# One more pair as seven products, one bank through four of them, the sums' first loads on another queue, and a reordered opening

## The chip, the cores and the metric

The kernel runs on one core of a Trainium2 chip. The time is the device time in microseconds (us) of one execution. It was measured in three runs. One further execution was recorded by the profiler, and everything that is said below of single instructions comes from that record.

The engines are named as the profile names them: PE is the matrix engine (TensorE), PEld its weight loads, DVE the vector engine, ACT the scalar engine, POOL the GpSimd engine, and SP the engine that here only issues DMAs. Each has its own queue of instructions and works it off in order. A DMA is issued by an instruction of some engine (SPq, POOLq, ACTq in the profile) and lands later; who needs its data waits for its semaphore.

## The reference

The reference is two layers of an encoder with width 1024 over 512 positions, all float32. In each layer four token mixers (latent attention, a Fourier transform, differential attention, a gated linear recurrence) run beside each other on one normalized input, their results are gated, summed and projected into the residual. Then comes the part that this case is mostly about, the feed-forward network (FFN) of width 2816:

```python
for l in range(DEPTH):                       # 2 layers
    ...
    h2 = rmsnorm(x, ln_ffn[l])
    ...
    x = x + (jax.nn.silu(g_part) * u_part) @ w_down[l]
```

`g_part` and `u_part` are the two halves of `h2 @ w_gate_up[l]`.

## The kernel before

The activations are kept transposed, as 8 tiles of 128 channels x 512 positions. Every float32 factor is split into two parts, `hi` and `lo`, in a format that PE multiplies fast: ACT writes `hi`, DVE writes `lo` as the difference (`split`, lines 121 and 122). A product is then three matmuls, hi x hi, hi x lo and lo x hi (lines 141 to 143 for a plain gemm, line 1066 for the seven products).

**Opening.** SP loads the first weight `hf00` in two cuts with `x` tile 0 between them, then the seven other x tiles, then the second weight `hf01` and more. The first gemm (`hf00`) consumes the x tiles as they come and are split into `hhm` and `hlm`. Then come `hf01`, `hq0`, `hg0`. `ssx` (line 188) is the sum of squares for the norm, two matmuls of true float32.

**FFN.** The 22 column tiles of the gate and the 22 of the up projection go as 22 pairs `j`. The string `SEVEN` says how pair j is computed:

- "8", an ordinary pair (`eight`): two gemms of 8 k-tiles x 3 matmuls of 128x512, so 48 matmuls.
- "7" (`seven`): the pair is seen as a 2 x 2 block product (gate and up columns by the two halves of the channels, times two halves of the channels by two halves of 256 positions) and is computed with seven products instead of eight, in the manner of Strassen and Winograd. Each product is 4 k-tiles x 3 matmuls of 128x256, so 84 matmuls in all. The products are named by what moves through PE: `T1` to `T4` are sums of the activations, made once for each layer (`right_sums`), and `B11`, `B21`, `B22` are plain blocks. The stationary factors are the weights `a11`, `a12`, `a22` and the sums of weights `s1` to `s4`.

`sums(j)` makes the weights of a seven. Three loads on SP bring `wr_f` (512 KB, two blocks), `s31` (512 KB, the first half of a sum) and `a22` (256 KB). One load on POOL then adds 512 KB more onto `s31` in memory (`accum_op`), so that `s31` holds two sums. It has to wait until the first load of `s31` has landed. From there DVE makes `s24` with two adds, and five splits follow: `one` (of `wr_f`, 1024 wide), `v24` (of `s24`, 1024 wide), `v1` and `v3` (the two halves of `s31`), and `v22` (of `a22`). `s31` has two buffers, so the load for pair j + 2 waits until the last reader of pair j's `s31` is done. In the trace `s31`, `s24` and so on are named without their numbers: `s_f` is `s31_f` and `s24_f`, `a_f` is `a22_f`, `vh_f` and `vl_f` are the hi and lo of the 512-wide splits, `wh_f` and `wl_f` of the 1024-wide ones.

The results of a seven go through three PSUM banks, `fa` (`r1`), `fb` (`r2`) and `fc` (`r3`). P1 below is the product of `a11` and P2 that of `a12`. The last two products of a seven, T4 and B22, with what follows (`finish`), are put off into the next seven, where `rest()` calls them. `hidden` multiplies gate and up and splits the result into `ah` and `al`. After 8, 8 and 6 pairs comes a piece of the down projection: eight gemms (`d`) over the pairs of the block.

The order in which instructions stand in each engine's queue is made by a scheduler from the order of the program and from priorities: `tc.high_priority(AHEAD)` in `sums` and `weight` moves loads and splits forward by 156 places. What stands where is fixed when the program is built, not at run time.

Of the kernel before, what the change touches and what calls it, by code (L numbers as in the profile page):

```python
# [11 lines left out]
F32 = mybir.dt.float32  # L12
# [16 lines left out]
LOG_EXP = "natural_log_exp_and_others"  # L29
WL, WR = 3, 2  # L30
LAYERS = range(L)
SEVEN = "8888887777777777777777"
AHEAD = 156
ORDER = "ccbccchhhchhcbchcghcchcchzccczccbccccccchgcgccchbbbcbhcgbzcbbcbccbgghcbgcgcbcccghchghchzhbccccbccccgcccccczhgcgbgchcgcccccccggggggbgcggggbcbbggcbbcbhcccbccbccccccccccccccccccbchccgbgggbchcbbbbbbhbbb"
PE = 8
PM = 4
# [26 lines left out]
def body(tc, io):  # L63
# [7 lines left out]
    with pool("const") as cl, pool("hp") as hp, pool("wp", WL) as wp, pool("vals", side="right") as cp, \  # L71
# [2 lines left out]
            pool("pq", 2, space=bass.MemoryType.PSUM) as pq:  # L74


        ident = cl.tile([P, P], F32, name="ident")
        make_identity(nc, ident)
        ones = cl.tile([P, P], F32, name="ones")
        V.memset(ones, 1.0)  # L80
        blk64 = cp.tile([P, P], F32, name="blk64")
        V.memset(blk64, 0.0)
        V.memset(blk64[0:64, 0:64], 1.0)
# [5 lines left out]
        xpool = [None]  # L89
        x = []  # L90

        def load_x(src, who):
            xpool[0] = pool(f"x{who}", side="right")
            px = xpool[0].__enter__()
            x[:] = [px.tile([P, S], F32, name=f"x{who}_{k}") for k in range(KD)]
            return [lambda k=k: nc.sync.dma_start(x[k], src[k]) for k in range(KD)]

        def drop_x():
            xpool[0].__exit__(None, None, None)
# [2 lines left out]
        def tmp(shape, tag="t", dt=F32, bufs=None, name="t"):  # L102
            return tp.tile(shape, dt, tag=tag, name=name, bufs=bufs)
# [21 lines left out]
            A.activation(hi, src, AF.Copy, scale=g)  # L125
            V.scalar_tensor_tensor(lo, src, g, hi.bitcast(F32), op0=ALU.mult, op1=ALU.subtract)

        def weight(src, n, name, cuts=(), between=None):
            raw = rp.tile([P, 1024], F32, tag="wr", name=f"wr_{name}")
            hi = wp.tile([P, 1024], F32R, tag="wh", name=f"wh_{name}")  # L130
            lo = wp.tile([P, 1024], F32R, tag="wl", name=f"wl_{name}")
            with tc.high_priority(AHEAD):
                for a, b in zip((0,) + cuts, cuts + (n,)):
                    nc.sync.dma_start(raw[:, a:b], src[:, a:b])
                    split(hi[:, a:b], lo[:, a:b], raw[:, a:b])
                    if between:
                        between.pop()()
            return hi, lo
# [87 lines left out]
        xs = nc.dram_tensor("x_mid", (KD, P, S), F32).ap()  # L226
        for l in LAYERS:
            lam_init = 0.8 - 0.6 * math.exp(-0.3 * l)
            pk = cp.tile([P, PK_N], F32, tag="pk", name=f"pk{l}")
            tc.keep_in_program_order(nc.scalar.preload_act_table_set(LOG_EXP))  # L230
            nc.scalar.dma_start(pk, io["pk"][l])


            if l == LAYERS[0]:
                with tc.high_priority(1000):
                    loads = load_x(io["x"], "in")
                    w0 = weight(io["w_z"][l, 0], 1024, "hf00", (256,), [loads[1], loads[0]])
                    for load in loads[2:]:
                        load()
            else:  # L240
                w0 = weight(io["w_z"][l, 0], 1024, "hf00")
            with pool(f"mo{l}") as mo, pool(f"mx{l}") as mp:
                hh, hl, scale, normed = prenorm(pk[:, PK_MIX:PK_MIX + 8], f"m{l}")
                first = [gemm(None, hh, hl, "hf00", w0)]
                r = scale()
                for c, name in ((1, "hf01"), (4, "hq0"), (6, "hg0")):
                    first.append(gemm(io["w_z"][l, c], hh, hl, name))
                sig0 = mp.tile([P, 3, S], F32, name="sig0")
                for j in range(2):
                    mul(sig0[:, j], first[j], r)  # L250
# [769 lines left out]
            with pool(f"fa{l}") as fa, pool(f"ff{l}") as fp, ps_pool(f"fr{l}", 2) as fr:  # L1020
# [48 lines left out]
                def sums(j):  # L1069

                    src = io["w_gu"][l, j]
                    with tc.high_priority(AHEAD):
                        raw = rp.tile([P, 1024], F32, tag="wr", name=f"wr_f{j}")
                        nc.sync.dma_start(raw, src[:, :1024])
                        s31 = fp.tile([P, 1024], F32, tag="s31", name=f"s31_f{j}", bufs=2)
                        nc.sync.dma_start(s31, src[:, 512:1536])
                        a22 = fp.tile([P, 512], F32, tag="a22", name=f"a22_f{j}", bufs=2)
                        nc.sync.dma_start(a22, src[:, 1536:])  # L1080
                        nc.gpsimd.dma_start(s31, src[:, 1024:], accum_op=ALU.add)

                        def pair(src, n):
                            if n == 1024:
                                hi = wp.tile([P, n], F32R, tag="wh", name=f"wh_f{j}")
                                lo = wp.tile([P, n], F32R, tag="wl", name=f"wl_f{j}")
                            else:
                                hi = fp.tile([P, n], F32R, tag="vh", name=f"vh_f{j}", bufs=4)
                                lo = fp.tile([P, n], F32R, tag="vl", name=f"vl_f{j}", bufs=4)
                            split(hi, lo, src)  # L1090
                            return hi, lo

                        one = pair(raw, 1024)
# [24 lines left out]

                def seven(j):
                    a11, a12, a22, s1, s2, s3, s4 = sums(j)  # L1120
                    gs = fp.tile([P, S], F32, tag="gs", name="gs")
                    us = fp.tile([P, S], F32, tag="us", name="us", bufs=2)
                    r1 = acc_psum(f"fa{j}")
                    product(r1, a11, B11, True)
                    c1 = tmp([P, H], "ps", name="c1")
                    A.activation(c1, r1[:, :H], AF.Copy)
                    rest()
                    r2 = fr.tile([P, S], F32, tag="r2", name=f"fb{j}")
                    r3 = acc_psum(f"fc{j}")
                    uu = tmp([P, 2, H], "n0", name="uu", bufs=1)  # L1130
                    product(r2, s2, T2, True)
                    add(uu[:, 0], c1, r2[:, :H])
                    product(r3, s1, T1, True)
                    product(r1, a12, B21, False)
                    A.activation(gs[:, :H], r1[:, :H], AF.Silu)
                    product(r2, s3, T3, False)
                    add(uu[:, 1], c1, r2[:, :H])
                    add(us[:, H:], uu[:, 1], r3[:, :H])

                    def finish():  # L1140
                        product(r2, a22, T4, False)
                        add(us[:, :H], c1, r2[:, :H])
                        product(r3, s4, B22, False)
                        add(gs[:, H:], uu[:, 0], r3[:, :H])
                        A.activation(gs[:, H:], gs[:, H:], AF.Silu)
                        hidden(j, gs, us, -1.0)

                    left.append(finish)

                def eight(j):  # L1150

                    t = [fp.tile([P, S], F32, tag=n, name=n, bufs=b) for n, b in (("gs", 1), ("us", 2))]
                    pr = []
                    for i in range(2):
                        if 2 * j + i < len(raw):
                            mul(t[i], raw[2 * j + i], r)
                            pr.append(t[i])
                        else:
                            pr.append(gemm(half_gu(2 * j + i), hh, hl, f"f{2 * j + i}"))
                        rest()  # L1160
                    A.activation(t[0], pr[0], AF.Silu)
                    if pr[1] is not t[1]:
                        mul(t[1], pr[1], t[0])
                        ah[j] = fa.tile([P, S], F32R, tag=f"ah{j % 8}", name=f"ah{j}")
# [148 lines left out]
```

## Time and profile before

| | us |
|---|---|
| median of 3 runs | 1725.94 (1723.2 to 1726.93) |
| profiled execution, its time | 1724.95 |
| profiled execution, its span | 1723.2 |
| PE busy | 1697.8 |
| PEld busy | 1422.5 |
| DVE busy | 1179.0 |
| ACT busy | 808.8 |
| POOL busy | 43.0 |

The span runs from the first to the last instruction; the time of an execution also holds what lies around it. A row of a time order has the start, the duration, the engine, the line, the operation with its output, an arrow and its inputs, the shape, the count, and in brackets the idle time ahead of it with the instruction that ended it. A group of instructions has its total busy time and the mean in ns. The chain of work that ended last is followed back from the last instruction. A row of DMA issues ends in the time from issue to landing.

### The profile page before, as it was taken

The numbers are of one execution on the slowest core, as the hardware profiler recorded it, in microseconds if no ns is written. First come the engines' busy times: TensorE is split into PE (matmuls) and PEld (weight loads), VectorE is DVE, ScalarE is ACT, GpSimd is POOL, SyncE is SP. The second block draws the span as 40 slices with busy tenths as digits, with TensorE's granted clock in tenths as the row PEclk, the third lists the DMA queues.
The fourth block names the chain that finished last, engine by engine and source line by source line (L and its number), as shares of the span: only waits on it lengthen the run. The fifth ranks groups of instructions, "written<-read, shape, count | busy, mean of one in ns | idle before, by whom it ended". The sixth has DMA issues, their size and how long they took to land.

```text
span 1723.2 us, 25722 instructions
## 1 busy us (share of the span) xinstructions
PE 1697.8 (99%) x10220; PEld 1422.5 (83%) x10220; DVE 1179.0 (68%) x1979; ACT 808.8 (47%) x1352; POOL 43.0 (2%) x68
## 2 busy tenths in 40 slices
PE   8999999999999999999999999999999999999999
PEld 6787778877787989989887777788777788899897
DVE  8858775457769647748677687754667695487473
ACT  7374353456555424525453743534564453254251
POOL 1000000000000000000000000000000000000000
PEclk9999999999999999999999999999999999999999
DMA  5222203332262435644442221142323624365443
GB/s 193 64 80 86 74 26 115 105 99 86 87 201 100 138 110 161 170 122 126 133 136 58 87 74 62 43 119 97 110 75 111 189 87 140 118 177 145 127 115 104
DMA packets 62473, 191.58 MB, mean 111 GB/s; under 512 B 7953, under 2 KB 9361, under 8 KB 62353
## 3 DMA queue, kind: packets, MB, share of 16 engines
q1 hardware_dynamic: 56304, 170.10, 30.4%
q0 software_dynamic: 5760, 19.42, 6.2%
q8 instruction: 80, 1.31, 0.3%
q10 hardware_dynamic: 288, 0.43, 0.1%
q14 instruction: 41, 0.33, 0.1%
HBM read 179.42 MB, written 4.19 MB: 107 GB/s over the span
## 4 chain that ended last, share of the span: by engine, by line
PE 87%; DVE 7%; ACT 3%; DMA 2%; issue 1%; SPq 0%; POOLq 0%; ACTq 0%; DVEq 0%
PE fb L1066 8%; PE g L142 6%; PE g L141 6%; PE g L143 6%; PE fc L1066 5%; PE fa L1066 5%; PE d L141 5%; PE d L143 5%; PE d L142 5%; PE f L142 3%; PE f L141 3%; PE f L143 3%; DMA s_f<-in_w_gu 2%; PE av L942 1%; PE sm L909 1%; PE hf L142 1%
## 5 line engine op out<-in xcount | busy, mean ns | idle before, releaser
L141 PE MATMUL g<-hhm,wh_g 128*128 128x512 f32 x512 | 202.0, 394 | 0.0
L143 PE MATMUL g<-hhm,wl_g 128*128 128x512 f32 x512 | 201.5, 394 | 0.0
L142 PE MATMUL g<-hlm,wh_g 128*128 128x512 f32 x512 | 201.5, 394 | 0.0
L143 PE MATMUL d<-ah,wl_d 128*128 128x512 f32 x352 | 136.9, 390 | 0.5 <-DVE wl_d L122 0.5
L141 PE MATMUL d<-ah,wh_d 128*128 128x512 f32 x352 | 137.2, 392 | 0.0
L142 PE MATMUL d<-al,wh_d 128*128 128x512 f32 x352 | 137.1, 390 | 0.0
L122 DVE TENSOR_TENSOR wl_g<-wr_g,wh_g 128x1024 fp32r<-128x1024 f32 x64 | 78.3, 1223 | 73.8 <-ACT wh_g L121 73.8
L121 ACT ACTIVATE wh_g<-wr_g 128x1024 fp32r<-128x1024 f32 x64 | 67.7, 1058 | 115.4 <-PE g L142 80.1
L142 PEld LDWEIGHTS g<-hlm,wh_g 128*128 128x128 f32 x512 | 96.3, 188 | 20.4 <-issue 1.5
L141 PEld LDWEIGHTS g<-hhm,wh_g 128*128 128x128 f32 x512 | 96.3, 188 | 20.2 <-issue 0.8
L143 PEld LDWEIGHTS g<-hhm,wl_g 128*128 128x128 f32 x512 | 96.3, 188 | 20.0 <-issue 0.8
L121 ACT ACTIVATE wh_d<-wr_d 128x1024 fp32r<-128x1024 f32 (+1 forms) x48 | 47.5, 989 | 111.7 <-PE d L142 85.5
L118 DVE TENSOR_TENSOR xm<-xm,d 128x512 f32<-128x512 f32 x48 | 33.0, 688 | 88.9 <-PE d L143 88.8
L121 ACT ACTIVATE wh_f<-wr_f 128x1024 fp32r<-128x1024 f32 x50 | 53.0, 1059 | 79.1 <-PE d L142 35.0
L121 ACT ACTIVATE vh_f<-s_f 128x512 fp32r<-128x512 f32 x64 | 40.1, 630 | 103.4 <-PE fb L1066 63.8
L910 DVE TENSOR_REDUCE nm<-sm 128x1 f32<-128x512 f32 x64 | 43.8, 689 | 51.3 <-PE sm L909 50.9
L143 PEld LDWEIGHTS d<-ah,wl_d 128*128 128x128 f32 x352 | 66.1, 188 | 14.9 <-DVE wl_d L122 1.4
L141 PEld LDWEIGHTS d<-ah,wh_d 128*128 128x128 f32 x352 | 66.0, 188 | 14.9 <-ACT ah L121 1.9
L142 PEld LDWEIGHTS d<-al,wh_d 128*128 128x128 f32 x352 | 66.1, 188 | 14.0 <-DVE al L122 1.2
L1066 PE MATMUL fb<-th,vh_f 128*128 128x256 f32 x256 | 75.7, 296 | 0.4 <-DVE uu L118 0.3
L1066 PE MATMUL fa<-hhf,wl_f 128*128 128x256 f32 x256 | 72.7, 284 | 0.0
L1066 PE MATMUL fa<-hlf,wh_f 128*128 128x256 f32 x256 | 72.5, 283 | 0.0
(444 smaller groups left out, 4845.6 us busy)
## 6 DMA issues: line engine op xcount, KB each, us to landing
wr_g<-in_w_g SPq DMA_DIRECT2D x64, 512.0 KB, 3.6
wr_f<-in_w_gu SPq DMA_DIRECT2D x50, 512.0 KB, 3.5
s_f<-in_w_gu SPq DMA_DIRECT2D x32, 512.0 KB, 4.5
s_f<-in_w_gu POOLq DMA_DIRECT2D x32, 512.0 KB, 5.4
wr_d<-in_w_d SPq DMA_DIRECT2D x32, 512.0 KB, 3.5
wr_b<-in_w_b SPq DMA_DIRECT2D x16, 512.0 KB, 3.4
wr_o<-in_w_o SPq DMA_DIRECT2D x16, 512.0 KB, 3.5
a_f<-in_w_gu SPq DMA_DIRECT2D x32, 256.0 KB, 3.0
```

Of the source, the lines that this page charges most:

```text
L118: V.tensor_tensor(out, a, b, op=ALU.add)
L121: A.activation(hi, src, AF.Copy)
L122: V.tensor_tensor(lo, src, hi.bitcast(F32), op=ALU.subtract)
L141: T.matmul(ps, lh, rh, start=first, stop=False)
L142: T.matmul(ps, lh, rl, start=False, stop=False)
L143: T.matmul(ps, ll, rh, start=False, stop=last)
L909: T.matmul(ps, qs[0:96, t * P:(t + 1) * P], ks[0:96], start=True, stop=True)
L910: V.tensor_reduce(nm[:, j:j + 1], ps, axis=AX.X, op=ALU.max, negate=True)
L942: T.matmul(av[e * 64:e * 64 + 64], vv[:, b, 2 * i + e], pts[i][e][:, b].rearrange("p t q -> p (t q)"), start=t == 1 and b == 0, stop=b == ...
L1066: T.matmul(ps[:, :H], lh[:, c], rh, start=first and k == 0 and n == 0, stop=k == Q - 1 and n == 2, skip_group_check=True)
```

## The change

1. `SEVEN` has five ordinary pairs at its start instead of six, so each layer has 17 sevens.
2. In `seven` P1 goes into `fb` (before: `fa`), and its result is copied by ACT (`c1`). P2 goes alone into `fa`, and DVE adds `c1` for the first half of the gate. Then come T4 and B22 of the pair before. T2, T3 and T4 go on accumulating on `fb`, and after each of them ACT copies what it holds (`cc[:, 0]`, `cc[:, 1]` and the first half of `us`). DVE adds that to what is in `fc`. In before, the four sums were made by DVE adds with `c1` (`uu`). Additions on DVE that read PSUM go from 5 to 3 in each seven, and what ACT reads of PSUM or of their result (copies and `silu`) from 3 to 6.
3. `gs` has two buffers instead of one, `us` one instead of two.
4. The first load of `s31` is issued by POOL, ahead of its accumulating load.
5. The opening: constants and the parameters `pk` come first, ten matmuls of a tile of ones with itself (`early`, 128x128, true float32) run first on PE, and SP loads the weight `hf01` in two cuts among the x tiles, in a fixed order.

The core of the diff:

```diff
-SEVEN = "8888887777777777777777"
+SEVEN = "8888877777777777777777"
+EARLY = 10
...
+        ones = cl.tile([P, P], F32, name="ones")
+        V.memset(ones, 1.0)
+        early = pq.tile([P, S], F32, tag="sc", name="early")
+        for _ in range(EARLY):
+            T.matmul(early[:, :P], ones, ones, start=True, stop=True)
...
-                    loads = load_x(io["x"], "in")
-                    w0 = weight(io["w_z"][l, 0], 1024, "hf00", (256,), [loads[1], loads[0]])
-                    for load in loads[2:]:
-                        load()
+                    loads = load_x(io["x"], "in", tc.keep_in_program_order)
+                    some = lambda *ks: lambda: [loads[k]() for k in ks]
+                    w0 = weight(io["w_z"][l, 0], 1024, "hf00", (256,), [some(1, 2, 3), some(0)],
+                                tc.keep_in_program_order)
+                    w1 = weight(io["w_z"][l, 1], 1024, "hf01", (512,), [some(6, 7), some(4, 5)],
+                                tc.keep_in_program_order)
...
-                        nc.sync.dma_start(s31, src[:, 512:1536])
+                        nc.gpsimd.dma_start(s31, src[:, 512:1536])
...
-                    gs = fp.tile([P, S], F32, tag="gs", name="gs")
-                    us = fp.tile([P, S], F32, tag="us", name="us", bufs=2)
+                    gs = fp.tile([P, S], F32, tag="gs", name="gs", bufs=2)
+                    c1 = tmp([P, H], "ps", name="c1")
                     r1 = acc_psum(f"fa{j}")
-                    product(r1, a11, B11, True)
-                    c1 = tmp([P, H], "ps", name="c1")
-                    A.activation(c1, r1[:, :H], AF.Copy)
+                    r2 = fr.tile([P, S], F32, tag="r2", name=f"fb{j}")
+                    product(r2, a11, B11, True)
+                    A.activation(c1, r2[:, :H], AF.Copy)
+                    product(r1, a12, B21, True)
+                    add(gs[:, :H], c1, r1[:, :H])
+                    A.activation(gs[:, :H], gs[:, :H], AF.Silu)
                     rest()
-                    r2 = fr.tile([P, S], F32, tag="r2", name=f"fb{j}")
+                    cc = tmp([P, 2, H], "n0", name="cc", bufs=1)
                     r3 = acc_psum(f"fc{j}")
-                    uu = tmp([P, 2, H], "n0", name="uu", bufs=1)
-                    product(r2, s2, T2, True)
-                    add(uu[:, 0], c1, r2[:, :H])
+                    product(r2, s2, T2, False)
+                    A.activation(cc[:, 0], r2[:, :H], AF.Copy)
                     product(r3, s1, T1, True)
-                    product(r1, a12, B21, False)
-                    A.activation(gs[:, :H], r1[:, :H], AF.Silu)
                     product(r2, s3, T3, False)
-                    add(uu[:, 1], c1, r2[:, :H])
-                    add(us[:, H:], uu[:, 1], r3[:, :H])
+                    A.activation(cc[:, 1], r2[:, :H], AF.Copy)
+                    us = fp.tile([P, S], F32, tag="us", name="us")
+                    add(us[:, H:], cc[:, 1], r3[:, :H])

                     def finish():
                         product(r2, a22, T4, False)
-                        add(us[:, :H], c1, r2[:, :H])
+                        A.activation(us[:, :H], r2[:, :H], AF.Copy)
                         product(r3, s4, B22, False)
-                        add(gs[:, H:], uu[:, 0], r3[:, :H])
+                        add(gs[:, H:], cc[:, 0], r3[:, :H])
```

The scheduler then puts the instructions in another order. DVE's queue between two sevens in the second block of a layer stood so in before; a row has the line, the operation, the output, an arrow, the inputs and the shape, `f12` is pair 12, and the last number of a name tells buffers apart:

```order
L122 TENSOR_TENSOR vl_f11_6277<-s31_f11_6256,vh_f11_6276 128x512
L122 TENSOR_TENSOR al9_6196<-us_6017,ah9_6195 128x512
L122 TENSOR_TENSOR wl_f11_6269<-s24_f11_6265,wh_f11_6268 128x1024
L122 TENSOR_TENSOR vl_f11_6281<-a22_f11_6258,vh_f11_6280 128x512
L118 TENSOR_TENSOR s24_f12_6399<-s31_f12_6390,wr_f12_6388 128x512
L118 TENSOR_TENSOR uu_6201<-c1_6165,fb10_6199 128x256
L118 TENSOR_TENSOR s24_f12_6399<-s24_f12_6399,wr_f12_6388 128x512
L118 TENSOR_TENSOR us_6151<-uu_6201,fc10_6200 128x256
```

and stands so now:

```order
L1128 SCALAR_TENSOR_TENSOR us_6201<-us_6201,gs_6098 128x512
L126 TENSOR_TENSOR s24_f12_6484<-s31_f12_6475,wr_f12_6473 128x512
L126 TENSOR_TENSOR s24_f12_6484<-s24_f12_6484,wr_f12_6473 128x512
L130 TENSOR_TENSOR vl_f11_6361<-s31_f11_6340,vh_f11_6360 128x512
L130 TENSOR_TENSOR al9_6293<-us_6201,ah9_6292 128x512
L130 TENSOR_TENSOR vl_f11_6365<-a22_f11_6342,vh_f11_6364 128x512
L126 TENSOR_TENSOR us_6336<-cc_6296,fc10_6297 128x256
L126 TENSOR_TENSOR gs_6368<-c1_6369,fa11_6370 128x256
```

The first row of the first piece is `v3` of pair 11, the last reader of `s31_f11`; it stood ahead of the two sums `s24` of pair 12 and stands behind them now. The add into `us` that reads bank `fc10` comes behind both in both.

The queues that issue the loads of a seven: before, on SP

```order
L1076 DMA wr_f12_6388<-in_w_gu 128x1024
L1078 DMA s31_f12_6390<-in_w_gu 128x1024
L1080 DMA a22_f12_6392<-in_w_gu 128x512
L1076 DMA wr_f13_6522<-in_w_gu 128x1024
L1078 DMA s31_f13_6524<-in_w_gu 128x1024
L1080 DMA a22_f13_6526<-in_w_gu 128x512
```

with the accumulating loads alone on POOL (line 1081), and now, on POOL:

```order
L1092 DMA s31_f11_6340<-in_w_gu 128x1024
L1095 DMA s31_f11_6340<-in_w_gu 128x1024
L1092 DMA s31_f12_6475<-in_w_gu 128x1024
L1095 DMA s31_f12_6475<-in_w_gu 128x1024
L1092 DMA s31_f13_6610<-in_w_gu 128x1024
L1095 DMA s31_f13_6610<-in_w_gu 128x1024
```

Line 1092 is the plain load and 1095 the accumulating one. Both are now in one queue, pair by pair, and SP keeps `wr_f` and `a22`.

At the start of the program SP's queue is now this, where before `hf01` stood behind all eight x tiles (`xin`) as one load:

```order
L142 DMA wr_hf00_119<-in_w_z 128x256
L104 DMA xin_0_111<-in_x 128x512
L142 DMA wr_hf00_119<-in_w_z 128x768
L104 DMA xin_1_112<-in_x 128x512
L104 DMA xin_2_113<-in_x 128x512
L104 DMA xin_3_114<-in_x 128x512
L142 DMA wr_hf01_132<-in_w_z 128x512
L104 DMA xin_4_115<-in_x 128x512
L104 DMA xin_5_116<-in_x 128x512
L142 DMA wr_hf01_132<-in_w_z 128x512
L104 DMA xin_6_117<-in_x 128x512
L104 DMA xin_7_118<-in_x 128x512
```

The two cuts of `hf01` come behind x tiles 3 and 5, and the last x tile is the last of them.

More of the change, by code (lines that the diff above doesn't have):

```diff
@@ L74, in body @@
             pool("pq", 2, space=bass.MemoryType.PSUM) as pq:
+        pk0 = cp.tile([P, PK_N], F32, tag="pk", name=f"pk{LAYERS[0]}")
+        tc.keep_in_program_order(nc.scalar.dma_start(pk0, io["pk"][LAYERS[0]]))
+        tc.keep_in_program_order(nc.scalar.preload_act_table_set(LOG_EXP))
+        ones = cl.tile([P, P], F32, name="ones")
[3 more added lines that the diff above has]
+            T.matmul(early[:, :P], ones, ones, start=True, stop=True)
         ident = cl.tile([P, P], F32, name="ident")
         make_identity(nc, ident)
-        ones = cl.tile([P, P], F32, name="ones")
-        V.memset(ones, 1.0)
         blk64 = cp.tile([P, P], F32, name="blk64")
@@ L90, in body, with load_x @@
         x = []
-        def load_x(src, who):
+        def load_x(src, who, keep=lambda i: i):
             xpool[0] = pool(f"x{who}", side="right")
@@ L95, in load_x @@
             x[:] = [px.tile([P, S], F32, name=f"x{who}_{k}") for k in range(KD)]
-            return [lambda k=k: nc.sync.dma_start(x[k], src[k]) for k in range(KD)]
+            return [lambda k=k: keep(nc.sync.dma_start(x[k], src[k])) for k in range(KD)]
         def drop_x():
@@ L126, in split_g, with weight @@
             V.scalar_tensor_tensor(lo, src, g, hi.bitcast(F32), op0=ALU.mult, op1=ALU.subtract)
-        def weight(src, n, name, cuts=(), between=None):
+        def weight(src, n, name, cuts=(), between=None, keep=lambda i: i):
             raw = rp.tile([P, 1024], F32, tag="wr", name=f"wr_{name}")
@@ L133, in weight @@
                 for a, b in zip((0,) + cuts, cuts + (n,)):
-                    nc.sync.dma_start(raw[:, a:b], src[:, a:b])
+                    keep(nc.sync.dma_start(raw[:, a:b], src[:, a:b]))
                     split(hi[:, a:b], lo[:, a:b], raw[:, a:b])
@@ L228, in body @@
             lam_init = 0.8 - 0.6 * math.exp(-0.3 * l)
-            pk = cp.tile([P, PK_N], F32, tag="pk", name=f"pk{l}")
-            tc.keep_in_program_order(nc.scalar.preload_act_table_set(LOG_EXP))
-            nc.scalar.dma_start(pk, io["pk"][l])
+            if l == LAYERS[0]:
+                pk = pk0
+            else:
+                pk = cp.tile([P, PK_N], F32, tag="pk", name=f"pk{l}")
+                tc.keep_in_program_order(nc.scalar.preload_act_table_set(LOG_EXP))
+                nc.scalar.dma_start(pk, io["pk"][l])
             if l == LAYERS[0]:
                 with tc.high_priority(1000):
-                    loads = load_x(io["x"], "in")
-                    w0 = weight(io["w_z"][l, 0], 1024, "hf00", (256,), [loads[1], loads[0]])
-                    for load in loads[2:]:
-                        load()
+                    loads = load_x(io["x"], "in", tc.keep_in_program_order)
[4 more added lines that the diff above has]
+                                tc.keep_in_program_order)
             else:
+                w1 = None
                 w0 = weight(io["w_z"][l, 0], 1024, "hf00")
@@ L246, in body @@
                 for c, name in ((1, "hf01"), (4, "hq0"), (6, "hg0")):
-                    first.append(gemm(io["w_z"][l, c], hh, hl, name))
+                    first.append(gemm(io["w_z"][l, c], hh, hl, name, w1 if c == 1 else None))
                 sig0 = mp.tile([P, 3, S], F32, name="sig0")
@@ L1150, in eight @@
                 def eight(j):
-                    t = [fp.tile([P, S], F32, tag=n, name=n, bufs=b) for n, b in (("gs", 1), ("us", 2))]
+                    t = [fp.tile([P, S], F32, tag=n, name=n, bufs=b) for n, b in (("gs", 2), ("us", 1))]
                     pr = []
```

## The prediction

> **What bounds the kernel now.** I read the page first, then the chain of work that ended last, then the time order of PE, DVE and the queues in the FFN.
>
> ```profile
> span 1723.2 us, 25722 instructions
> PE 1697.8 (99%) x10220; PEld 1422.5 (83%) x10220; DVE 1179.0 (68%) x1979; ACT 808.8 (47%) x1352; POOL 43.0 (2%) x68
> PE 87%; DVE 7%; ACT 3%; DMA 2%; issue 1%; SPq 0%; POOLq 0%; ACTq 0%; DVEq 0%
> ```
>
> TensorE (PE) is the bound, with 87% of the chain. So an edit gains only what it takes out of PE's own row of matmuls, and it loses whatever makes PE wait. POOL issues few instructions, among them the accumulating loads of the sevens. The FFN of the chain shows the unit of work:
>
> ```profile
> 669.00 1.44 PE fa L1066 x12
> 670.43 1.44 PE fb L1066 x12
> 671.88 1.44 PE fa L1066 x12
> 673.32 3.00 PE fb L1066 x23
> ```
>
> One product of twelve 128x256 matmuls takes 1.44 us, so a "seven" is 7 x 1.44 = 10.08 us of PE.
>
> **The change, part by part.**
>
> *One more seven per layer.* An "eight" is two gemms of 24 matmuls 128x512. The next rows give their spacing, and they serve the opening too:
>
> ```profile
> 6.59 0.79 PE L141 MATMUL hf<-hhm,wh_hf 128*128 128x512 f32 x1 [6.59 <-ACT hhm L125]
> 12.99 0.59 PE L142 MATMUL hf<-hlm,wh_hf 128*128 128x512 f32 x1
> 13.41 0.40 PE L143 MATMUL hf<-hhm,wl_hf 128*128 128x512 f32 x1
> 20.24 1.02 PE L188 MATMUL ssx<-ss,ones 128*128 128x512 f32 x2
> 22.25 0.39 PE L141 MATMUL hq<-hhm,wh_hq 128*128 128x512 f32 x1
> 23.84 0.39 PE L142 MATMUL hq<-hlm,wh_hq 128*128 128x512 f32 x1
> ```
>
> From 22.25 to 23.84 are seven steps, 0.227 each; an eight is 48 x 0.227 = 10.89 us. A pair gains 0.81 and there is one per layer: **-1.6 us**.
>
> *The fourth product's wait.* In before, T4 writes the bank `fb` that the DVE add into `uu` still reads. The add stands in DVE's queue behind weight sums, so T4 starts late in every seven. The first and the last place with a gap ahead of T4, in time order, and the groups of the page:
>
> ```profile
> 588.38 0.28 PE L1066 MATMUL fb<-th,wh_f 128*128 128x256 f32 x1
> 588.58 0.38 PE L1066 MATMUL fb<-th,vh_f 128*128 128x256 f32 x1
> 1675.38 0.28 PE L1066 MATMUL fb<-tl,wh_f 128*128 128x256 f32 x1
> 1675.59 0.39 PE L1066 MATMUL fb<-th,vh_f 128*128 128x256 f32 x1
> L1066 PE MATMUL fb<-th,vh_f 128*128 128x256 f32 x256 | 75.7, 296 | 0.4 <-DVE uu L118 0.3
> L1066 PE MATMUL fa<-hlf,wh_f 128*128 128x256 f32 x256 | 72.5, 283 | 0.0
> ```
>
> A late first matmul is longer, and over 32 sevens the group of T3 and T4 is 75.7 - 72.5 = 3.2 us above its equal. The gap ahead of it is 0.2 instead of 0.12, in sixteen such places from 588 to 1675, some 2.3 us with the larger ones (0.48 at most). Together 5.5 us. In the change T4 waits for an ACT copy made right after T3, and P1 and P2 of the next pair (2.88 us) lie between. The copy costs about this:
>
> ```profile
> 671.67 0.36 ACT L1135 ACTIVATE gs<-fa 128x256 f32<-128x256 f32 x1
> 671.93 0.62 ACT L121 ACTIVATE vh_f<-a_f 128x512 fp32r<-128x512 f32 x1
> 673.35 0.38 ACT L1126 ACTIVATE c<-fa 128x256 f32<-128x256 f32 x1 [0.80 <-PE fa L1066]
> ```
>
> Three more copies are 1.1 us per seven on an engine that is 47% busy. They are hidden, but T3 waits for the copy of T2 with only T1's 1.44 us between, and a copy that lands behind a 1.06 us split would use that up. I take **-5 us**, with bounds 0 and -5.5.
>
> *The opening.* PE runs at 0.427 per matmul (6.41 over 15 from 6.59 to 12.99) and at 0.227 from 13.41. The second gemm's weight came last, so 24 of its matmuls and the ssx pair (1.0 us) stand behind the first gemm, and hq starts at 22.25. The bytes up to there are the same in the change (3.1 MB):
>
> ```profile
> 6.00:13.00 7.00, 6.41 (x14) 4.30 (x15) 6.40 (x10) 7.00 (x12) 0.00 (x0) 1.00 1.03 393
> ```
>
> At 393 GB/s they still end at about 12.3; x7 then comes last, and its split ends near 13.9. By then the two gemms have run interleaved, and some 18 matmuls (4.1 us) and ssx (1.0 us) are left, so hq starts at about 19.0, a gain of 3.3 if the clock is open by then. The ten early matmuls take about 0.43 each (estimate from the slow spacing), 4.3 us in all, and can run before the first data comes, that is before 6.59. If they bring the clock forward only partly the gain is about 2.2, and 0 if nothing moves. I take **-2.8**.
>
> [...]
>
> *The first load of `s31` on POOL's queue.* This decides the forecast. Each seven needs a sum loaded in two steps, a plain 512 KB load and an accumulating one that waits for the first to land:
>
> ```profile
> 660.34 0.33 SPq L1078 DMA_DIRECT2D s_f<-in_w_gu  x1
> 665.15 0.86 POOL L1081 DMA_DIRECT2D s_f<-in_w_gu  x1 [10.37 <-DVE us L118]
> s_f<-in_w_gu SPq DMA_DIRECT2D x1, 512.0 KB, 4.3
> s_f<-in_w_gu POOLq DMA_DIRECT2D x1, 512.0 KB, 5.4
> s_f<-in_w_gu SPq DMA_DIRECT2D x32, 512.0 KB, 4.5
> s_f<-in_w_gu POOLq DMA_DIRECT2D x32, 512.0 KB, 5.4
> ```
>
> The single-issue rows belong to the two issues above them: 660.34 + 4.3 = 664.6 landed, 0.55 later POOL issues, and 5.4 later the sum is there: 10.2 us per pair of loads. In before this hides, because DVE reads in this order:
>
> ```profile
> 670.07 0.69 DVE L122 TENSOR_TENSOR vl_f<-s_f,vh_f 128x512 fp32r<-128x512 f32 x1
> 670.78 0.33 SPq L1078 DMA_DIRECT2D s_f<-in_w_gu  x1
> 673.55 0.68 DVE L118 TENSOR_TENSOR s_f<-s_f,wr_f 128x512 f32<-128x512 f32 x1
> 674.48 0.68 DVE L118 TENSOR_TENSOR s_f<-s_f,wr_f 128x512 f32<-128x512 f32 x1
> ```
>
> The last reader of pair n's buffer (the v3 split, 670.07) ends, SP reloads it at once (670.78) for pair n+2, and only then come the sums of pair n+1 (673.55). In the changed order DVE does the sums of n+1 **first**, then v3 of n. With two buffers that closes a loop: sums of n+1 wait for their loads, v3 of n waits behind them, the loads for n+2 wait for v3 of n, and the sums of n+2 wait for those. One turn costs:
> - sums and v3 on DVE: 0.2 to notice the landing, 0.6 + 0.6 + 0.69 by the rows' spacing: 2.1 us
> - release to issue: 0.05 (670.76 to 670.78 on SP; up to 0.55 on POOL)
> - landing to the next issue 0.55, the accumulating load 5.2 (5.4 and 5.0 in the two single-issue rows)
> - the plain load on POOL. Before doesn't show it for this tile. Of these two rows, the first is of all `s_f` loads on both queues, the second of the only plain loads of this size that POOL issues, `dft`, four of 516 KB, two at a time; the third is a single accumulating one:
>
> ```profile
> DMA to landing us min/median/max: 3.0/5.1/10.2
> DMA to landing us min/median/max: 3.9/4.5/4.9
> s_f<-in_w_gu POOLq DMA_DIRECT2D x1, 512.0 KB, 5.0
> ```
>
> The lower end for it is 3.0 (SP's best), the upper 4.9. I take 4.0, near the shortest of POOL's own, since here it is alone but for a 256 KB load.
>
> The sum is 2.1 + 0.05 + 4.0 + 0.55 + 5.2 = **11.9 us a turn**, against 10.08 of PE work. Behind v3 on DVE stand the al and v22 splits and the add that empties bank `fc`, for which PE's B22 waits: 3.7 us after the sums can start. Walk a block of eight sevens, with its first product at 0. The first seven has no predecessor to finish (7.2 us), then each takes 10.08, so B22 of the second, third and fourth seven is due at 21.6, 31.7 and 41.8. Ahead of the adds that release them stand the sums of the fourth, fifth and sixth seven, which so must start by 17.9, 28.0 and 38.1. v3 of the second seven goes into the buffer that T1 of the first reads until 4 x 1.44 = 5.8; with 0.2 to notice, 0.62 on ACT and 0.69 on DVE it ends at 7.3. So the fourth sums start at 7.3 + 9.8 = 17.1 (in time), the fifth at 29.0 (1.0 late), and every later one 1.8 further behind. The late places are the sums of the last four sevens: 1.0 + 3 x 1.8 = 6.5. A block of six has 1.0 + 1.8 = 2.8; the first block's three sevens have none. That is 9.3 per layer, **+18.6 us**. Bounds: turns of 10.6 or less give 0; 11.3 gives about 9; 12.5 (the plain load at 4.5) about 28; 12.9 (at 4.9) about 34.
>
> [...]
>
> SP's queue only loses a load per seven, and on POOL nothing stands behind these waits but the loads of the next seven.
>
> Sum, against the profiled execution's own 1724.95 (1.75 above its span, 1.0 below the median of 1725.94): 1724.95 - 1.6 - 5 - 2.8 + 18.6 = **1734.2 us**.
>
> **The rivals.**
> - *The loads keep up* (not slower). Point of decision: a turn of 10.6 us. If the plain load on POOL takes SP's shortest 3.0 and the accumulating one its shortest 5.0, a turn is 2.1 + 0.05 + 3.0 + 0.55 + 5.0 = 10.7, and the loop costs under 1 us: 1724.95 - 9.4 + 0 to 1 = 1715.5 to 1716.5. For it: in before SP's load is asked for 1.2 us behind a `wr_f` load of 512 KB and is slowed by it, and in the change it isn't. Against it: the four POOL loads never took under 3.9.
> - *Just over*: a turn near 11.2 to 11.4, with 7 to 11 us of stall: 1722.5 to 1727, no change that could be told.
> - *The loads crowd each other*: a turn of 12.3 to 12.9, since SP's `wr_f` and `a_f` loads run beside both, and the DVE order leaves no slack to take it up: 1740 to 1750.
> - *The opening does nothing*: the sum is 2.8 higher, 1737. This goes with each case above.
>
> **How the numbers follow.** The forecast (1730 to 1738) has 0.38; crowding 0.19; just over 0.15; keeping up 0.28. A difference under 0.2%, 3.5 us, is about what a measurement of this kernel can't tell from no change. Faster than 1722.5 takes the rival of loads that keep up and a little of "just over": 0.30. Within: 0.14. Slower: 0.56. For 8 in 10 the range must reach both the fast rival and the crowded one: 1715 to 1746.
>
> **What would show it.** In the FFN of the changed kernel PE must wait in front of B22 (bank `fc`, for the DVE add into `us`), and from the fifth seven of each block on, about 1.8 us each; DVE must sit idle for the accumulating DMA of `s_f`; the pairs of loads must take 9.8 us from the first issue to the second landing. T4 must start without a gap, and hq at about 19. If POOL's plain load lands in under 3.2 us, or the sums' wait is shorter than the slack, the loop is harmless and the kernel is faster by about 9 us.

## The result, and the profile after

The changed kernel takes **1773.11 us** (median of 4 runs, 1764.61 to 1774.77) against 1724.86 for the kernel before (the median of four runs by now): 1.0269 of its time, 95% interval 1.0234 to 1.0304. It was forecast slower, at 1734.2 and at most 1746; it is slower by 48 us, not by 9. The profiled execution has these rows on its page:

```profile
span 1771.2 us, 26023 instructions
PE 1715.4 (97%) x10312; PEld 1445.3 (82%) x10312; DVE 1162.8 (66%) x1932; ACT 847.7 (48%) x1464; POOL 63.4 (4%) x104
PE 77%; DVE 8%; issue 8%; ACT 3%; DMA 3%; POOL 0%; DVEq 0%; SPq 0%; POOLq 0%; ACTq 0%
```

PE's share of the chain falls from 87% to 77%, and `issue`, the time for which the profile names no cause, rises from 1% to 8%. In the list of PE's own waits one row stands out that the kernel before does not have (engine and tile that wait, what for: us in total, times, longest):

```profile
PE fc L1080 <- DVE us L126: 37.9, 17, 4.3
```

This is the wait that the forecast named, PE's B22 before the DVE add into `us`, 17 times instead of 12 and twice as long in all. The windows from the first down projection to the second (eight sevens) and from the second to the third (six sevens), before and then after, show that the sevens hold nearly all of it (length, busy time of each engine with its instructions, granted clock, DMA share, GB/s):

```profile
596.80:721.80 125.00, 124.68 (x855) 115.52 (x854) 82.41 (x125) 50.27 (x78) 6.96 (x8) 1.00 0.54 148
721.80:829.10 107.30, 107.00 (x710) 97.84 (x709) 69.09 (x103) 41.43 (x63) 3.49 (x4) 1.00 0.42 119
```

```profile
597.20:740.10 142.90, 131.84 (x866) 122.65 (x865) 78.84 (x113) 60.31 (x104) 11.36 (x16) 0.95 0.49 133
740.10:856.00 115.90, 108.08 (x699) 99.30 (x698) 62.03 (x87) 45.90 (x78) 5.68 (x8) 0.97 0.40 112
```

The first is 17.9 us longer, the second 8.6. Of the 17.9, 10.7 are time in which PE is idle, and 7.2 are more busy time, at a granted clock of 0.95. In the second layer the same two windows are 18.1 and 3.1 us longer (142.8 and 110.5 against 124.7 and 107.4), so the four hold 47.7 of the 48 us.

The loop is seen one turn at a time on DVE (the two sums in one row, v3, the add into `us`, and the split of `wr_f`), on POOL and SP, with the time to landing of the single issues at 679.45, 683.87 and 682.18:

```profile
677.13 1.42 DVE L126 TENSOR_TENSOR s_f<-s_f,wr_f 128x512 f32<-128x512 f32 x2 [4.06 <-issue]
678.47 0.68 DVE L130 TENSOR_TENSOR vl_f<-s_f,vh_f 128x512 fp32r<-128x512 f32 x1
680.27 0.41 DVE L126 TENSOR_TENSOR us<-cc,fc 128x256 f32<-128x256 f32 x1
680.93 1.22 DVE L130 TENSOR_TENSOR wl_f<-wr_f,wh_f 128x1024 fp32r<-128x1024 f32 x1
691.16 1.42 DVE L126 TENSOR_TENSOR s_f<-s_f,wr_f 128x512 f32<-128x512 f32 x2 [5.90 <-issue]
```

```profile
679.45 0.56 POOL L1092 DMA_DIRECT2D s_f<-in_w_gu  x1 [8.04 <-DVE vl_f L130]
683.87 0.87 POOL L1095 DMA_DIRECT2D s_f<-in_w_gu  x1 [3.86 <-DMA s_f<-in_w_gu]
693.48 0.56 POOL L1092 DMA_DIRECT2D s_f<-in_w_gu  x1 [8.74 <-DVE vl_f L130]
```

```profile
682.18 0.33 SPq L1090 DMA_DIRECT2D wr_f<-in_w_gu  x1
```

```profile
s_f<-in_w_gu POOLq DMA_DIRECT2D x1, 512.0 KB, 4.1
s_f<-in_w_gu POOLq DMA_DIRECT2D x1, 512.0 KB, 7.2
wr_f<-in_w_gu SPq DMA_DIRECT2D x1, 512.0 KB, 4.3
```

From sums to sums are 691.16 - 677.13 = 14.0 us: 2.3 until POOL issues, 4.1 for the plain load, 0.3 to the next issue, **7.2 for the accumulating load**, 0.1 until DVE starts. The forecast had 11.9 with 5.2 in that place. The five turns of this block, from one plain load to the next, are 14.8, 12.8, 14.0, 13.8 and 14.2 us. DVE sits idle 5.90 us in front of the sums, and behind them stand the instructions that PE waits for. The row gives `issue` as the end of that wait, so the profile doesn't name its cause; that it is the accumulating load is read from the times, 683.87 + 7.2 = 691.1 and 691.16.

### The profile page after: what moved, and what is told of

Read it like the earlier page. It is cut to its first block, busy times and chain, and to the rows that moved or that the text cites. A ratio compares the mean times of both kernels' runs of the same rounds, so it can differ in the third digit from the quotient of the medians.

```text
span 1771.2 us, 26023 instructions
## 1 busy us (share of the span) xinstructions
PE 1715.4 (97%) x10312; PEld 1445.3 (82%) x10312; DVE 1162.8 (66%) x1932; ACT 847.7 (48%) x1464; POOL 63.4 (4%) x104
## 4 chain that ended last, share of the span: by engine, by line
PE 77%; DVE 8%; issue 8%; ACT 3%; DMA 3%; POOL 0%; DVEq 0%; SPq 0%; POOLq 0%; ACTq 0%
PE g L150 6%; PE g L149 6%; PE g L151 6%; PE fb L1080 6%; PE d L150 5%; PE d L149 5%; PE d L151 5%; PE fc L1080 3%; PE f L150 3%; PE f L149 3%; PE f L151 3%; DMA s_f<-in_w_gu 2%; PE o L150 2%; PE o L151 2%; PE o L149 2%
## 5 line engine op out<-in xcount | busy, mean ns | idle before, releaser
L126 DVE TENSOR_TENSOR s_f<-s_f,wr_f 128x512 f32<-128x512 f32 x68 | 47.0, 691 | 99.0 <-issue 76.0
L1080 PE MATMUL fc<-hhf,wh_f 128*128 128x256 f32 x136 | 43.3, 318 | 37.9 <-DVE us L126 37.9
L149 PEld LDWEIGHTS d<-ah,wh_d 128*128 128x128 f32 x352 | 66.0, 188 | 14.2 <-ACT ah L129 0.6
L1080 PE MATMUL fb<-tl,vh_f 128*128 128x256 f32 x272 | 76.9, 283 | 0.0
```

Of the source, the lines that this page charges most:

```text
L126: V.tensor_tensor(out, a, b, op=ALU.add)
L149: T.matmul(ps, lh, rh, start=first, stop=False)
L1080: T.matmul(ps[:, :H], lh[:, c], rh, start=first and k == 0 and n == 0, stop=k == Q - 1 and n == 2, skip_group_check=True)
```

## The experiments

Each time is a median, with its ratio to runs of the kernel before on the same chip.

| run | us | ratio (95%) |
|---|---|---|
| changed kernel | 1773.11 | 1.0269 (1.0234 to 1.0304) |
| edge | 1719.05 | 0.9975 (0.9966 to 0.9985) |
| sp_load | 1750.51 | 1.0152 (1.0137 to 1.0168) |
| pool_load | 1723.06 | 0.9995 (0.9985 to 1.0004) |
| open_only | 1726.21 | 1.0011 (1.0001 to 1.0020) |
| wr_late | 1749.76 | 1.0137 (1.0119 to 1.0155) |
| fill | 1770.78 | 1.0268 (1.0252 to 1.0283) |
| edge_old_open | 1718.86 | 0.9968 (0.9957 to 0.9980) |
| edge_sp | 1718.95 | 0.9973 (0.9962 to 0.9984) |
| bank_only | 1753.68 | 1.0168 (1.0153 to 1.0183) |
| bank_edge | 1723.66 | 0.9992 (0.9983 to 1.0001) |
| edge_wr | 1721.19 | 0.9982 (0.9972 to 0.9991) |
| five_only | 1723.33 | 0.9994 (0.9985 to 1.0003) |

### edge: one edge of order against the loop

```diff
-                        add(s24[:, :512], s31[:, 512:], raw[:, 512:])
+                        first = add(s24[:, :512], s31[:, 512:], raw[:, 512:])
+                        if v3s:
+                            tc.add_manual_dep(first.ins, v3s[-1].ins.name, mybir.DependencyInfo(
+                                mybir.DependencyClass.NoSync, mybir.DependencyReason.DATA), reason="order")
...
                         v3 = pair(s31[:, :512], 512)
+                        v3s.append(last[-1])
```

`last` holds the DVE instructions of the splits. The edge adds no wait on another engine; it sets which of two instructions stands first in DVE's queue, and the scheduler then places the rest.

> The changed kernel with one edge added to the order of DVE's queue: the sums of pair n+1 stand behind the v3 split of pair n, as before the change; loads, products and opening stay as changed. Theory L (the order on DVE closes a loop through the two s31 buffers): the waits of PE for the DVE add into us fall from 17 of together 37.9 us to a few under 1 us each, the clock's half-speed windows in the FFN go with them, and the time falls by 40 to 55 us, to 1716 to 1730. Theory Q (both loads of a sum in one POOL queue are slow by themselves): the order changes little, time stays above 1755. Theory R (the reordered additions matter less than slower accumulating loads): in between, 1735 to 1755.

1719.05 us: 54 us are gone, and the kernel is faster than before. The row of waits and the issues of POOL in the second block:

```profile
PE fc L1080 <- DVE us L126: 3.5, 3, 1.5
```

```profile
659.82 0.56 POOL L1094 DMA_DIRECT2D s_f<-in_w_gu  x1 [5.10 <-DVE vl_f L130]
663.57 0.85 POOL L1097 DMA_DIRECT2D s_f<-in_w_gu  x1 [3.19 <-DMA s_f<-in_w_gu]
669.90 0.56 POOL L1094 DMA_DIRECT2D s_f<-in_w_gu  x1 [5.49 <-DVE vl_f L130]
```

From load to load are 669.90 - 659.82 = 10.08 us, which is PE's own time for a seven. DVE's queue from v3 to the add into `us` is now:

```profile
668.91 0.69 DVE L130 TENSOR_TENSOR vl_f<-s_f,vh_f 128x512 fp32r<-128x512 f32 x1 [0.62 <-ACT vh_f L129]
669.96 0.69 DVE L126 TENSOR_TENSOR s_f<-s_f,wr_f 128x512 f32<-128x512 f32 x1 [0.35 <-DMA s_f<-in_w_gu]
670.57 0.68 DVE L130 TENSOR_TENSOR al<-us,ah 128x512 fp32r<-128x512 f32 x1
671.17 0.68 DVE L130 TENSOR_TENSOR vl_f<-a_f,vh_f 128x512 fp32r<-128x512 f32 x1
671.77 0.69 DVE L126 TENSOR_TENSOR s_f<-s_f,wr_f 128x512 f32<-128x512 f32 x1
672.37 0.41 DVE L126 TENSOR_TENSOR us<-cc,fc 128x256 f32<-128x256 f32 x1
```

v3 stands first again, and the second sum has also moved, behind the al and v22 splits. In the two traces PE, ACT, POOL and SP have the same instructions in the same order; only DVE's order differs. Theory L holds: the order of a few instructions in one queue is what the change costs. Theories Q and R fall.

### sp_load and pool_load: the queue of the first load

sp_load is the changed kernel with the load back on SP, pool_load the kernel before with the load on POOL; each differs by this line alone:

```diff
-                        nc.gpsimd.dma_start(s31, src[:, 512:1536])
+                        nc.sync.dma_start(s31, src[:, 512:1536])
```

> The changed kernel with the first load of s31 back on SP's queue; DVE's order stays as changed (sums ahead of v3). Theory L: the loop stays, its turn is shorter only by what SP's load is shorter than POOL's (about 0.5 us of 14), so 1755 to 1770. Theory Q: the loss is gone, 1715 to 1730.

> The kernel before with only the first load of s31 moved to POOL's queue; DVE's order stays as before (v3 ahead of the sums). Theory L: no loop, so within 4 us of the kernel before (1721 to 1729). Theory Q: slower by 20 us or more.

pool_load is 0.9995 of before: without the loop the queue costs nothing. sp_load is 1.0152: with the loop SP's queue doesn't take the loss away. It does take more of it than was expected (1750.5, expected from 1755). The row of waits of sp_load:

```profile
PE fc L1080 <- DVE us L126: 20.1, 11, 3.4
```

By the ratios some 20 of the 46 us hang on the queue, though only while the loop turns: in the second block the five turns take 12.9 us on average instead of 13.9, with plain loads of 3.1 to 3.6 us (3.5 to 4.2 in the changed kernel) and accumulating loads of 6.1 to 7.9 (6.5 to 8.1). Where a loop sets the pace, each tenth in its turn is paid once per seven; the queue is one of the terms of the turn, not the cause of the loop.

### bank_only and bank_edge: the new `seven` by itself

bank_only is the kernel before with nothing but the new `seven` (its products, copies and buffers, as in the diff above); bank_edge adds the edge of order to it.

> The kernel before with the new products and buffers of seven alone (one bank through four products, gs 2 and us 1 buffers); six ordinary pairs, SP's load and the opening as before. DVE's order has the sums ahead of v3 here too. Theory L: the loss is this part's alone and comes close to that of the changed kernel with SP's load (1750.5), less one seven per layer: 1743 to 1752. If the extra seven or the opening had a share in the loss: under 1740.

> The same with the one added edge of order. It prices the one bank without its loop: the 5 us of T4's late starts were forecast, less what accumulating loads beside wr_f still cost: 1719 to 1722. If T4's wait is worth nothing: 1724.

bank_only shows 1.0168, and this row of waits:

```profile
PE fc L1066 <- DVE us L118: 23.4, 13, 3.2
```

So the loop comes with the rewritten products and their buffers alone: here too DVE has the sums of the next pair (677.34) ahead of v3 (678.68). Why the scheduler orders them so was not tested. At 1753.7 it lies 2 us above the range given. bank_edge is 0.9992, at 1.4 us of gain rather than the 3 to 6 that were expected, and its interval reaches to 1.0001. Its groups and its row of waits say why:

```profile
L1066 PE MATMUL fb<-th,vh_f 128*128 128x256 f32 x256 | 72.9, 285 | 0.0
L1066 PE MATMUL fb<-tl,vh_f 128*128 128x256 f32 x256 | 72.4, 283 | 0.0
```

```profile
PE fc L1066 <- DVE us L118: 4.3, 4, 1.9
```

T4's late starts are gone (75.7 before, 72.9 now, beside an equal at 72.4), but 4.3 us of new waits stand in front of B22.

### wr_late: the accumulating load without a neighbour

SP's `wr_f` load of pair n + 1 waits for the landing of the accumulating load of pair n; nothing else differs from the changed kernel:

```diff
-                        nc.sync.dma_start(raw, src[:, :1024])
+                        wr = nc.sync.dma_start(raw, src[:, :1024])
+                        if summed:
+                            tc.add_manual_dep(wr.ins, summed[-1].ins.name, mybir.DependencyInfo(
+                                mybir.DependencyClass.Sync, mybir.DependencyReason.DATA), reason="wr")
...
-                        nc.gpsimd.dma_start(s31, src[:, 1024:], accum_op=ALU.add)
+                        summed.append(nc.gpsimd.dma_start(s31, src[:, 1024:], accum_op=ALU.add))
```

> The changed kernel with one wait more: SP's wr_f load of pair n+1 is asked for only when the accumulating load of pair n has landed, so that the two no longer run beside each other; DVE's order stays as changed. Theory C (the accumulating load takes 7.2 instead of 5.2 us because it now runs beside wr_f): it falls to 5.0 to 5.6, a turn of the loop from 14.0 to about 12.0, and the time from 1773 to 1733 to 1748. Theory P (it is slow because the plain load ahead of it is in the same POOL queue, or because it is asked for 0.28 instead of 0.56 us after that one's landing): it stays near 7 and the time above 1765.

POOL's issues, SP's `wr_f`, and the times to landing of the two POOL issues at 675.95 and 680.36:

```profile
675.95 0.56 POOL L1097 DMA_DIRECT2D s_f<-in_w_gu  x1 [6.91 <-DVE vl_f L130]
680.36 0.87 POOL L1100 DMA_DIRECT2D s_f<-in_w_gu  x1 [3.85 <-DMA s_f<-in_w_gu]
688.09 0.56 POOL L1097 DMA_DIRECT2D s_f<-in_w_gu  x1 [6.86 <-DVE vl_f L130]
```

```profile
685.74 0.33 SPq L1092 DMA_DIRECT2D wr_f<-in_w_gu  x1
```

```profile
s_f<-in_w_gu POOLq DMA_DIRECT2D x1, 512.0 KB, 4.1
s_f<-in_w_gu POOLq DMA_DIRECT2D x1, 512.0 KB, 5.3
```

With no `wr_f` load beside it the accumulating load takes 5.3 us, though it stands behind the plain load in POOL's queue, is asked for as soon after it as in the changed kernel, and the loop still turns. The turn is 688.09 - 675.95 = 12.1. Theory C holds and P falls. The time falls by 23 us, to 2 us above the range: at the ends of the blocks, where loads of `wr_d` come in, the accumulating load still takes over 7, and B22 still waits 23.7 us in all. Another 6 us lie between the third down projection of the first layer and the first of the second (627.9 us, 621.8 in before), where the clock is at half speed for 6.8 us at 928 and again at 1447.

### fill: the clock

The granted clock of the changed kernel drops to half in ten windows in the FFN. Two neighbouring ones:

```profile
692.42:695.83 3.41, 1.06 (x9) 1.06 (x10) 3.41 (x7) 0.75 (x2) 0.56 (x1) 1.00 0.30 107
695.83:699.25 3.42, 3.42 (x19) 3.42 (x18) 2.86 (x5) 1.83 (x4) 0.86 (x1) 0.50 0.86 287
```

PE works for 1.06 us of the first because it waits for B22's release; the second is granted 0.50. Its matmuls stand 0.21 us apart instead of 0.12, some 1.5 us of loss in each such window. Ten of them would be 15 us. fill puts work of no use into the wait (and keeps B22's first matmul behind it):

```diff
                         A.activation(us[:, :H], r2[:, :H], AF.Copy)
+                        if j in (10, 11, 12, 13, 14, 18, 19, 20):
+                            fill = sc_psum("fill")
+                            for _ in range(14):
+                                tc.keep_in_program_order(T.matmul(
+                                    fill[:, :H], hh[0][:, :P], hh[0][:, :H], start=True, stop=True))
                         product(r3, s4, B22, False)
```

> The changed kernel with 14 more matmuls of 128x256 (1.7 us, result not read) between T4 and B22 in eight sevens of each layer, just where PE waits for the DVE add into us. Theory K (each half-speed window of the clock that follows such a wait costs its 1.4 us): PE is busier in the windows, most of the ten half-speed windows in the FFN go, and the time falls by 8 to 14 us, to 1759 to 1765. Theory L (the loop of loads and sums sets the pace, and PE's slow stretches only eat into its next wait): the time stays within 4 us of 1773, whether the half-speed windows go or not.

The half-speed windows in the FFN fall from ten to two, and the time is 1770.78 (1.0268, where the changed kernel has 1.0269). The row of waits:

```profile
PE fc L1080 <- DVE us L126: 18.6, 13, 2.4
```

PE now works through 27 us more of matmuls, waits 19 us less, and hardly anything comes of it. The total alone can't settle why, since some of the filler may stand in PE's way and use up what the clock gains. The block of eight in the first layer says more. It has one half-speed window instead of four, some 4.5 us of loss less, and is 2.4 us shorter (140.5 against 142.9). Its five turns take 66.4 us in all instead of 69.6, and the accumulating loads in them 33.8 instead of 36.7: the block follows its loads. All four windows are 5.2 us shorter, less than K's 8 to 14, and between the layers 2.7 us are lost again, where this execution has a half-speed stretch at 942. While the loop of loads sets the pace, a slow clock takes its time, or most of it, out of PE's next wait. Theory L holds, K falls.

### open_only and edge_old_open: the opening

open_only is the kernel before with the new opening; edge_old_open is edge with the old one.

> The kernel before with only the new opening. The changed kernel starts hq 1.3 us earlier, but reaches the output projection of layer 0 0.7 us later, with a half-speed stretch of 6.8 us of the clock from 64.4 us that before doesn't have. If the phase of the clock's windows set by the early matmuls is the cause, this kernel shows the same stretch and is within 2 us of before (1723 to 1727). If the opening's gain holds by itself: 1721.5 to 1723.5.

> The kernel with the added edge of order, and with the opening of before in place of the new one. By the run with the new opening alone (1.0011 of before) the opening is worth nothing or costs up to 2 us: 1716 to 1719. If it gains its 1.3 us here: 1720 to 1721.

open_only is 1.0011 (just clear of 1), edge_old_open 0.9968 beside edge's 0.9975 on another chip: the opening is worth nothing or costs up to 2 us. The clock in open_only, early and in the mixers of the second layer:

```profile
4.80:8.20 3.40, 2.06 (x9) 0.99 (x7) 2.97 (x13) 3.14 (x7) 0.00 (x0) 1.00 1.03 384
8.20:15.00 6.80, 6.24 (x15) 4.56 (x15) 6.80 (x12) 6.80 (x13) 0.00 (x0) 0.50 0.78 291
916.10:919.50 3.40, 2.83 (x43) 2.28 (x42) 2.99 (x9) 1.69 (x7) 0.00 (x0) 1.00 0.53 146
919.50:926.30 6.80, 6.70 (x68) 6.05 (x72) 6.21 (x15) 0.98 (x2) 0.00 (x0) 0.50 0.02 8
```

The column of the clock reads 1.00 wherever no drop is recorded, also at the start of the program, where the kernel before has its matmuls 0.427 us apart; an opening is therefore read from the spacing, and here from the drop at 8.20. By that drop the clock of open_only was open before 8.20, where the spacing in before stays at 0.427 until 13.41. But PE worked for only 2.06 of the 3.40 us ahead of 8.20, and from there to 15.00 it was granted 0.50 (in the changed kernel one wait of this stretch, 1.06 us ahead of 8.04, is for the split of an x tile). Behind 3.40 us with 2.83 us of work the clock is at 0.50 again from 919.50 to 926.30. I expected the stretch at 64 us, which is the same place of the first layer. In the profiles with the new opening it comes at 64 or 65 (changed kernel, sp_load, fill), between 916 and 943 (open_only, wr_late, fill) or not at all (edge, edge_sp, edge_wr), and bank_only has it at 936 with the old opening; I have no run that controls it, and none that shows a phase set by the early matmuls.

### edge_sp, five_only, edge_wr

> The kernel with the added edge of order, and with the first load of s31 on SP's queue as before. Theory L: without the loop the queue hardly matters, 1716 to 1722.

> The kernel before with five ordinary pairs instead of six and nothing else. By 48 matmuls of 0.227 against 84 of 0.12 it gains 0.8 us per layer; the seven added brings one more late T4 and an accumulating load early in the block: 1722 to 1725.

> The kernel with the edge of order and with SP's wr_f load asked for only after the accumulating load of the pair before has landed. If the 3.5 us of waits left in the edge kernel come from accumulating loads of 6.7 us beside wr_f, they go: 1714 to 1717. If wr_f then comes too late for its own split: 1719 to 1726.

edge_sp (0.9973) is as fast as edge: again the queue is free. five_only changes `SEVEN` alone: 0.9994, 1.7 us less by the medians, as 1.6 was worked out, though its interval reaches to 1.0003. edge_wr, the edge with wr_late's wait, gains nothing: 1721.19. Most of its accumulating loads in mid-block fall to 5.2 to 5.7 us (the slowest still take 8.0 in the first layer and 7.1 in the second), and 2.9 us of waits remain, spread over six places instead of three; the second guess, that `wr_f` then comes late itself, fits but wasn't shown.

edge, edge_sp, edge_old_open and edge_wr are faster than the kernel before, by 0.18 to 0.32%, each with an interval that stays below 1.

## Why the prediction was right in kind and wrong in size

**One more seven:** -1.6 worked out, -1.7 measured (five_only), though its interval, up to 1.0003, does not exclude no change.

**T4's late starts:** the mechanism held. In the changed kernel the first group below, of T3 and T4, is nearly as short as its equal:

```profile
L1080 PE MATMUL fb<-th,vh_f 128*128 128x256 f32 x272 | 77.7, 286 | 0.2 <-ACT cc L1148 0.2
L1080 PE MATMUL fb<-tl,vh_f 128*128 128x256 f32 x272 | 76.9, 283 | 0.0
```

Yet 5 us of net gain was too much even without the loop. bank_edge has 1.4, not clear of no change, since 4.3 us of waits in front of B22 take its place; the forecast priced the new wait only for the loop.

**The opening:** -2.8 was forecast from a clock open for good; it measures 0 to +2. No run shows the -2.8: behind the early matmuls the clock opened, but was at 0.50 again from 9.75 to 13.16 (changed kernel) and from 8.20 to 15.00 (open_only). The step that failed is "so hq starts at about 19.0". The three windows after the early matmuls, and the row of hq:

```profile
2.93:6.34 3.41, 3.41 (x15) 2.91 (x14) 2.06 (x12) 1.76 (x4) 0.00 (x0) 1.00 0.98 341
6.34:9.75 3.41, 1.90 (x6) 0.87 (x6) 3.04 (x9) 3.31 (x7) 0.00 (x0) 1.00 1.02 365
9.75:13.16 3.41, 3.17 (x8) 2.33 (x8) 3.41 (x6) 3.41 (x7) 0.00 (x0) 0.50 1.04 404
```

```profile
21.04 0.39 PE L149 MATMUL hq<-hhm,wh_hq 128*128 128x512 f32 x1
```

The recorded drop is 9.75 to 13.16; the two windows ahead of it are counted back by its length. Matmuls start 0.40 us apart at 6.18 and 6.58 and 0.23 apart at 9.33 and 9.56, so the clock opened in between. PE worked for 3.41 of 3.41 us in the first window and for 1.90 in the second, and the drop at 9.75 followed. hq came at 21.04, 1.2 us earlier than before instead of 3.3. From 64.37 to 71.19 the changed kernel's clock is at 0.50 and that of the kernel before at 1.00, and its first output projection (`o`) starts 0.7 us late (468.06 against 467.39); edge, which has no such stretch, starts it at 466.07, 1.3 us early. The forecast asked only whether the clock is open by then, not whether it stays open while PE waits for x tiles. Up to 1692.52 the drops recorded in the changed kernel last 3.41 us or twice that (6.83), and 9.75, 64.37 and 668.52, where three of them begin, lie 54.62 and 604.15 us apart, which is 16 and 177 times 3.413.

**The loop:** the order on DVE, the two buffers, the place of the wait, the deadlines and the late sevens were as forecast, and edge shows that nothing else makes the loss. The step that failed is the term "the accumulating load 5.2". It was taken from two rows of before (5.4 and 5.0). A smaller one, the 0.2 us "to notice", is shown by no run; the turn above has 0.1 from the landing to DVE's start. The forecast asked what runs beside the plain load ("alone but for a 256 KB load"; it took 4.1, as it said) and not what runs beside the accumulating one. That one measures 7.2. SP's `wr_f` is asked for as soon as the split of the last `wr_f` has ended. In before these two rows show it:

```profile
668.33 1.23 DVE L122 TENSOR_TENSOR wl_f<-wr_f,wh_f 128x1024 fp32r<-128x1024 f32 x1
669.58 0.33 SPq L1076 DMA_DIRECT2D wr_f<-in_w_gu  x1
```

There the split ends at 669.56, 1.2 us ahead of v3 (670.76), so `wr_f` runs beside the plain load. In the changed order it ends 3.0 us behind v3 (682.15 and 679.16), so `wr_f` with its 512 KB is asked for 1.7 us ahead of the accumulating load (682.18 and 683.87) and runs beside that. wr_late takes this one load away and finds 5.3. The neighbour belongs to the new order of the products and not to the loop: edge has it too (accumulating load at 663.57, `wr_f` at 665.01, 6.3 us) and loses little by it.

By the forecast's own walk a turn of 14.0 makes the fourth sums start at 7.3 + 11.9 = 19.2, 1.3 us late, and adds 3.9 for each later seven: 1.3 + 4 x 3.9 = 16.9 in a block of eight and 1.3 + 2 x 3.9 = 9.1 in one of six, 52 us in both layers. The 37.9 us of waits and the ten half-speed windows (about 15) make nearly the same. With the opening at 0 the sum is 1724.95 - 6.6 + 52 = 1770, 3 us below the median. That it comes so near is in part luck: the second layer's block of six lost 3.1 us and not 9, since its last two accumulating loads took 5.6 and 5.1. In wr_late, with the term as forecast, the block of eight is 8.3 us longer than before:

```profile
597.40:730.70 133.30, 127.06 (x866) 118.05 (x865) 78.54 (x113) 60.30 (x104) 11.36 (x16) 0.99 0.53 142
```

The forecast had 6.5 less its gains for it. The four windows together are 20.5 us longer, where its loop had 18.6 before the gains.

The rival of loads that crowd each other was the right one, and it named `wr_f`, but its price had the wrong member: it let the plain load grow to 4.9 (it took 4.1) and left the accumulating one at 5.2, so it ended at a turn of 12.9. The rows for a larger bound were in the trace of before, where the landing of `s_f` loads reaches 10.2 us. I put the loop under the heading of the load's queue; pool_load and bank_only show that it belongs to the rewritten products.

## What to carry to other kernels

When an order changes, look for the last reader of each buffer that a load waits for, and ask what now stands ahead of it in its queue; if that waits for the same chain of loads one step on, there is a loop, and its turn has to be shorter than the work that covers it. Then place every other transfer of the cycle on the new time axis before taking a duration for a load: moving a reader moves the loads, and the neighbours change. While such a loop sets the pace, making PE faster, or its clock, gives little (2 us here).

## What the runs showed of the hardware that was not expected

- An accumulating DMA of 512 KB took 5.0 to 5.4 us in the first layer's second block, where no other load of that size ran beside it for long (before, wr_late), and 6.5 to 8.1 in the changed kernel beside one plain load of the same size, which itself took 4.3 to 6.1 (3.1 to 3.6 in wr_late). It isn't always so: in bank_edge, where `wr_f` is asked for 0.7 to 1.5 us behind the accumulating load, three of four took 5.4 to 6.0 and one 7.2, and `wr_f` took 5.2 to 6.8.
- POOL issued its accumulating load 0.28 us after the plain load had landed when both were its own (683.59 to 683.87), and 0.55 us when SP had issued the plain one (664.60 to 665.15, before).
- In the changed kernel the granted clock was 0.50 for 3.41 us after 3.41 us in which PE was 31% (692.42) or 56% (6.34) busy, and in open_only for 6.80 us after 3.40 us at 83% (916.10). In the kernel before PE was busy for 80% of the time from 64.37 to 71.19, and the granted clock stayed at 1.00, so these runs don't show what busy share goes with a drop.
